# A decoder layer on one core: the second norm written in a fixed order on all engines, between the first products of two gate/up pairs, and four left operands split inside the attention's last steps

## The chip, the cores and the metric

The kernel runs on one core of a Trainium2 chip. The time is the device time of one execution in microseconds (us); a lower one is better. TensorE is written PE, VectorE DVE, ScalarE ACT, GpSimd POOL, and SP is the engine that issues most of the loads.

## What is computed

One decoder layer on x of 512 tokens by 1024 features, all in fp32. An input norm and a projection feed four groups of attention heads; their outputs stand side by side in `mix` and go through `w_out`. Then, cut to what matters here:

```python
x = x + _rms_norm(mix @ w_out[l], attn_post_norm[l])
h = _rms_norm(x, ffn_pre_norm[l])
x = x + _rms_norm(_conv_ffn(h, ffn_w_gate[l], ffn_w_up[l], ffn_conv_w[l], ffn_conv_b[l], ffn_w_down[l]),
                  ffn_post_norm[l])
```

`_conv_ffn` multiplies h by `w_gate` and by `w_up` (1024 by 4096 each), runs a causal convolution of width 3 and a gelu on the gate branch, multiplies the two and goes through `w_down`. The first two lines, from `mix @ w_out` on, and the first products with `w_gate` and `w_up` are what the change touches.

## The kernel before

**Numbers as pairs.** Every matrix operand is held as two fp32r tiles, a rounded copy "hi" and the rest "lo". The copy is made by ACT (line 181 for weights, 1210 for activations), the rest by a DVE subtraction (lines 184, 1211). A product is three matmuls: hi·hi, hi·lo, lo·hi (lines 397 to 399 for the projections, 1263 to 1265 for gate and up).

**Gate and up.** The columns of `w_gate` and `w_up` are taken in 16 pairs, 1 MB of each per pair. One pair is multiplied by a seven-product scheme: the weights' blocks 11, 12, 21, 22 and sums of them are the *left operands* (`operand`, j from 0 to 6, two tiles of hi and two of lo each, 8 instructions on ACT and DVE for two operands), and blocks of h and sums of them, transposed on PE, are the *right operands* R["21"], R["11"], R["t3"], R["t1"], R["t2"], R["t4"], R["22"] (`right_operand`). The sums of weights ("combos") are POOL subtractions and additions of 128 x 512 on line 167: 8 per pair. A product is 24 matmuls.

**The order of the work.** Most of it is placed by a scheduler that goes by the order of issue and by priorities (`tc.high_priority`). The attention runs by a list of events; between them matmuls of the projections (`fill`) fill PE, and small jobs of the other engines wait in a queue (`later`, `pop`, `flush`). After the last event the program runs `flush()`, then the *rest of the output projection*: `out_rest(t, n)` for token block t (0 to 3) and half n (0, 1), 12 matmuls of 128 x 512 each, the last group of heads' share of `mix` among them. Its sums go into `part[t][n]` (line 1168). Four loads of x are issued from ACT's queue at line 1155.

**The second norm** (`second_norm(t)`, `rstd2`) stands behind that for each t: two squares on ACT (line 1176) over the halves of `part[t]`, a root on POOL (1182), a multiplication by the gain (1192, on POOL but for t = 0), the sum with x (1195, DVE), a square over all 1024 columns, a second root, and the multiplication by root and second gain (1198, DVE). Token blocks 0 and 1 give R["11"] and R["21"]; with them the first two products of pairs 0 and 1 run (`first_products`, twice). `other_operands` makes eight differences of the normalised blocks (line 1235, six on DVE and two on POOL, as `TS` says) and the other five right operands, and `other_products` runs the remaining products.

**Left operands at hand.** `W.spare` names two left operands (j = 0 and 1 of pair 0) that have tiles of their own; their 8 splits are popped after the attention. The other operands use slots in turn.

## Time and profile before

| | |
|---|---|
| median of 3 runs | 821.67 us (821.47 to 822.93) |
| the profiled execution | 821.43 us, its span 819.6 us, 1.83 us around the span |
| busy share of the span | PE 95%, DVE 80%, ACT 54%, POOL 42% |
| attention ends (last attention product) | about 265.8 us |
| rest of the output projection on PE | to 282.9 us |
| first gate/up product starts | 298.2 us |

The table's last three lines are read from the timeline of PE. A row of a timeline gives the start in us, the length of the whole group, the engine, the line, the operation, output <- input and the count; in brackets the engine's idle time before it and the instruction that ended this. A row of a window gives for each engine its busy time in the stretch, then the granted clock of PE as a share of full speed.

### The profile page before, as it was taken

The numbers are of one execution on the slowest core, as the hardware profiler recorded it, in microseconds if no ns is written. First come the engines' busy times: TensorE is split into PE (matmuls) and PEld (weight loads), VectorE is DVE, ScalarE is ACT, GpSimd is POOL, SyncE is SP. The second block draws the span as 40 slices with busy tenths as digits, with TensorE's granted clock in tenths as the row PEclk, the third lists the DMA queues.
The fourth block names the chain that finished last, engine by engine and source line by source line (L and its number), as shares of the span: only waits on it lengthen the run. The fifth ranks groups of instructions, "written<-read, shape, count | busy, mean of one in ns | idle before, by whom it ended". The sixth has DMA issues, their size and how long they took to land.

```text
span 819.6 us, 13498 instructions
## 1 busy us (share of the span) xinstructions
PE 781.0 (95%) x5079; PEld 711.5 (87%) x5079; DVE 659.2 (80%) x1126; ACT 445.7 (54%) x930; POOL 341.1 (42%) x314
## 2 busy tenths in 40 slices
PE   6999998999999769999999999999999999999996
PEld 5998886998878659988998998998998998998984
DVE  3547669777686999996797797797897987989867
ACT  5557656776776545645554454454354444444532
POOL 5236342337344657343343442451561561563102
PEclk9999998999999969999999999999999999999999
DMA  7274211406321403412114305206116025033112
GB/s 219 61 199 129 58 40 45 119 21 203 111 77 52 154 5 108 147 61 94 52 51 155 104 12 194 84 22 206 52 52 206 12 92 185 21 104 104 63 67 103
DMA packets 72921, 78.77 MB, mean 96 GB/s; under 512 B 7782, under 2 KB 58136, under 8 KB 72856
## 3 DMA queue, kind: packets, MB, share of 16 engines
q1 hardware_dynamic: 71032, 73.71, 29.4%
q10 hardware_dynamic: 1824, 4.20, 1.5%
q8 instruction: 40, 0.66, 0.3%
q14 instruction: 25, 0.20, 0.1%
HBM read 73.71 MB, written 2.10 MB: 92 GB/s over the span
## 4 chain that ended last, share of the span: by engine, by line
PE 62%; DVE 27%; DMA 3%; ACT 3%; issue 3%; POOL 1%; SPq 0%; ACTq 0%; DVEq 0%; POOLq 0%
DVE wu L184 10%; PE mm L397 5%; PE mm L398 4%; PE mm L399 4%; PE tr L398 4%; PE mm L1263 3%; PE mm L1265 3%; PE mm L1264 3%; PE tr L399 3%; PE tr L397 3%; PE sc L1265 3%; PE sc L1264 3%; PE sc L1263 3%; DVE y L1313 3%; PE tr L924 2%
## 5 line engine op out<-in xcount | busy, mean ns | idle before, releaser
L184 DVE TENSOR_TENSOR wu<-pair,wu 128x512 fp32r<-128x512 f32 x188 | 175.7, 970 | 17.1 <-ACT wu L181 16.7
L181 ACT ACTIVATE wu<-pair 128x512 fp32r<-128x512 f32 x188 | 108.6, 622 | 76.5 <-PE sc L1265 19.7
L1265 PE MATMUL mm<-fT,wu 128*128 128x256 f32 x488 | 138.4, 284 | 0.7 <-DVE wu L184 0.7
L1263 PE MATMUL mm<-fT,wu 128*128 128x256 f32 x488 | 138.3, 283 | 0.7 <-ACT mo L1294 0.7
L1264 PE MATMUL mm<-fT,wu 128*128 128x256 f32 x488 | 138.2, 283 | 0.0
L142 ACT ACTIVATE wu<-raw 128x512 fp32r<-128x512 f32 (+2 forms) x126 | 71.3, 609 | 79.1 <-PE sc L1265 29.1
L1264 PE MATMUL sc<-fT,wu 128*128 128x256 f32 x392 | 111.4, 284 | 0.0
L1263 PE MATMUL sc<-fT,wu 128*128 128x256 f32 x392 | 111.2, 284 | 0.0
L1265 PE MATMUL sc<-fT,wu 128*128 128x256 f32 x392 | 111.2, 284 | 0.0
L167 POOL TENSOR_TENSOR sum<-pair 128x512 f32<-128x512 f32 x32 | 48.4, 1515 | 141.2 <-DVE wu L147 60.7
L167 POOL TENSOR_TENSOR pair<-pair 128x512 f32<-128x512 f32 x64 | 104.5, 1643 | 2.0
L167 POOL TENSOR_TENSOR pair<-sum,pair 128x512 f32<-128x512 f32 x32 | 55.9, 1761 | 116.0 <-DVE wu L184 114.2
L147 DVE TENSOR_TENSOR wu<-raw,wu 128x512 fp32r<-128x512 f32 (+2 forms) x95 | 67.8, 728 | 37.4 <-ACT wu L142 37.0
L1263 PEld LDWEIGHTS mm<-fT,wu 128*128 128x128 f32 x488 | 93.6, 192 | 1.2 <-ACT mo L1294 0.9
L1265 PEld LDWEIGHTS mm<-fT,wu 128*128 128x128 f32 x488 | 93.6, 192 | 1.1 <-DVE wu L184 1.1
L1264 PEld LDWEIGHTS mm<-fT,wu 128*128 128x128 f32 x488 | 93.6, 192 | 0.3
L1263 PEld LDWEIGHTS sc<-fT,wu 128*128 128x128 f32 x392 | 75.5, 193 | 0.3
L1264 PEld LDWEIGHTS sc<-fT,wu 128*128 128x128 f32 x392 | 75.5, 192 | 0.4
L1265 PEld LDWEIGHTS sc<-fT,wu 128*128 128x128 f32 x392 | 75.3, 192 | 0.0
L892 POOL TENSOR_SCALAR P<-P,rc 128x128 f32<-128x128 f32 (+2 forms) x80 | 42.6, 552 | 75.0 <-DVE rc L990 29.5
L147 POOL TENSOR_TENSOR wu<-raw,wu 128x512 fp32r<-128x512 f32 (+2 forms) x31 | 42.8, 1384 | 55.1 <-ACT wu L142 48.9
L900 ACT ACTIVATE P<-P,mn 128x128 f32<-128x128 f32 (+2 forms) x96 | 52.0, 543 | 21.1 <-DVE mn L899 20.6
(317 smaller groups left out, 1993.1 us busy)
## 6 DMA issues: line engine op xcount, KB each, us to landing
pair<-in_ffn_w_gate_dram SPq DMA_DIRECT2D x16, 1024.0 KB
pair<-in_ffn_w_up_dram SPq DMA_DIRECT2D x16, 1024.0 KB, 5.3
raw<-in_ffn_w_down_dram SPq DMA_DIRECT2D x32, 512.0 KB, 3.8
raw<-in_w_in_dram SPq DMA_DIRECT2D x14, 512.0 KB, 3.8
raw<-in_w_out_dram SPq DMA_DIRECT2D x8, 512.0 KB, 4.2
raw<-in_w_in_dram SPq DMA_DIRECT2D x10, 256.0 KB, 2.9
x<-in_x_dram SPq DMA_DIRECT2D x4, 512.0 KB, 6.2
x<-in_x_dram ACTq DMA_DIRECT2D x4, 512.0 KB, 8.9
```

The lines of the kernel that those rows point to most:

```text
L142: self.nc.scalar.activation(box["h"][:, sl], box["r"][:, sl], AF.Copy)
L147: eng.tensor_tensor(box["l"][:, sl], box["r"][:, sl], f32(box["h"][:, sl]), op=ALU.subtract)
L167: self.nc.gpsimd.tensor_tensor(block(g, out), block(g, a), block(g, b), op=op)
L181: self.nc.scalar.activation(box["h"][g], block(g, src), AF.Copy)
L184: self.nc.vector.tensor_sub(box["l"][g], block(g, src), f32(box["h"][g]))
L397: pe.matmul(o, lh, rh, start=first, stop=False)
L398: pe.matmul(o, lh, rl, start=False, stop=False)
L399: pe.matmul(o, ll, rh, start=False, stop=last)
L900: act.activation(pi, pi, AF.Exp, bias=mn[:, i:i + 1], scale=-1.0, accum_out=sm[:, i:i + 1])
L1263: pe.matmul(o, wh, rh, start=first, stop=False, skip_group_check=True)
L1264: pe.matmul(o, wh, rl, start=False, stop=False, skip_group_check=True)
L1265: pe.matmul(o, wl, rh, start=False, stop=last, skip_group_check=True)
```

## The change

- `W.spare` has four operands: j = 0, 1 and also j = 2 ("21") and j = 3 (a sum) of pair 0. In the last part of the attention ("draining") `ask_ahead` queues their 16 splits, and five jobs are popped per event. The first four combos of pair 0 are made earlier.
- The x of token blocks 0 and 1 goes into four tiles `xm` by SP before; x of blocks 2 and 3 is loaded by SP. The loads of pair 1's up weights stand behind these.
- The rest of the output projection, the norm, and the first products are written out instruction by instruction, each of them kept in this order (`tc.keep_in_program_order`). Squares are taken per half (16 on ACT in place of 8 and 4 of double width); each root is three POOL instructions (`r` from the first half's sum, plus the second half's, to the power); the gain multiplication goes to POOL for n = 0 and to DVE for n = 1; all eight differences are on DVE. The differences, t3's, t1's and the further right operands stand between and inside products.
- `mix_pair`'s lo part is on DVE for the last group of heads.

The core of the diff:

```diff
-    W.spare = {W.early: None, W.early + 1: None}
+    W.spare = {W.early + n: None for n in (0, 1, 4, 5)}
...
-        (pool if MLO else vec).tensor_tensor(mixT[1][n], mo, f32(mixT[0][n]), op=ALU.subtract)
+        (pool if n < 6 else vec).tensor_tensor(mixT[1][n], mo, f32(mixT[0][n]), op=ALU.subtract)
...
+        draining = time > now + LAGC - 0.1
+        if draining and "out" not in seen:
+            fill_to("out")
+            flush()
+            W.ask_ahead()
         with tc.high_priority(HP):
             f()
-    fill_to("out")
+            if draining:
+                for _ in range(5):
+                    if side:
+                        pop()
...
+    def squares(t, n, src, c):
...
+        keep(act.activation(junk[:, 0:512], src, AF.Square, scale=1.0 / 32, accum_out=ss[:, n:n + 1]))
+        if n == 0:
+            keep(pool.tensor_scalar(r, ss[:, 0:1], 1.0, EPS, ALU.mult, ALU.add))
         else:
+            keep(pool.tensor_tensor(r, r, ss[:, 1:2], op=ALU.add))
+            keep(pool.tensor_tensor(r, r, mhalf[:, 0:1], op=ALU.pow))
+
+    def half_done(t, n):
+        adds[t, n]()
+        squares(t, n, part[t][n], 0)
+        keep((pool, vec)[n].tensor_tensor(part[t][n], part[t][n], half_of(gpost, n), op=ALU.mult))
+
+    def residual(t, n):
+        xh = half_of(x1[t], n)
+        keep(vec.scalar_tensor_tensor(xh, part[t][n], rms[t, 0][1], f32(xm[t][n]) if t < 2 else xh, ALU.mult, ALU.add))
+        squares(t, n, xh, 1)
+
+    def second_norm(t, n):
+        keep(vec.scalar_tensor_tensor(part[t][n], half_of(x1[t], n), rms[t, 1][1], half_of(gpre, n), ALU.mult, ALU.mult))
...
+    run_all(*(out_rest(t, n) for t in range(2) for n in range(2)))
+    half_done(0, 0)
+    half_done(0, 1)
+    half_done(1, 0)
+    residual(0, 0)
+    residual(0, 1)
+    half_done(1, 1)
+    W.keep = keep
+    run_all(out_rest(2, 0, keep), out_rest(3, 0, keep))
...
+    R["21"], to21 = right_operand([p[0][1], p[1][1]], tags, "M", keep)
+    run_all(g)
+    W.free(2)
+    R["11"], to11 = right_operand([p[0][0], p[1][0]], tags, "M", keep)
+    half_done(2, 1)
+    for f in to21:
+        f()
+    residual(2, 0)
+    half_done(3, 1)
+    residual(2, 1)
+    for f in to11:
+        f()
...
-    firsts = [first_products(tag) for tag in ("mm", "sc")]
-    with tc.high_priority(HN):
-        other_operands()
+    firsts = [first_products("mm", None, keep)]
+    for _ in range(4):
+        pop()
+    residual(3, 0)
+    residual(3, 1)
+    second_norm(2, 1)
+    second_norm(2, 0)
+    for _ in range(4):
+        pop()
+    less(p[0][0], p[2][0], p[0][0], keep)
+    less(p[2][0], p[2][1], p[2][0], keep)
+    firsts[0][2]()
+    second_norm(3, 0)
+    second_norm(3, 1)
+    less(p[1][0], p[3][0], p[1][0], keep)
+    less(p[3][0], p[3][1], p[3][0], keep)
+    todo = []
+
+    def third():
+        R["t3"], f = right_operand([p[2][0], p[3][0]], tags, "H", keep)
+        todo.extend(f)
+    firsts.append(first_products("sc", third, keep))
```

`product` calls `between` after a given number of its matmuls, so t3's transposes stand behind 18 of the 24 matmuls of the fourth product.

**PE, end of the attention.** `va` holds the last attention product (operands `PT`, `vs`), `mixh` and `mixl` the hi and lo of `mix`, `mm` and `sc` the accumulators of `out_rest`. Before:

```order
L1090 MATMUL va_498_3067<-PT_493_3032,vs_1821 128x128
L397 MATMUL mm_517_3179<-wu28_3043,mixh_479_2973 128x512
L398 MATMUL mm_517_3179<-wu28_3043,mixh_479_2973 128x512
L397 MATMUL mm_518_3193<-wu28_3043,mixh_479_2973 128x512
L398 MATMUL mm_518_3193<-wu28_3043,mixh_479_2973 128x512
L397 MATMUL sc_519_3207<-wu30_3129,mixh_479_2973 128x512
L398 MATMUL sc_519_3207<-wu30_3129,mixh_479_2973 128x512
L397 MATMUL sc_520_3221<-wu30_3129,mixh_479_2973 128x512
```

Now:

```order
L1104 MATMUL va_517_3149<-PT_509_3120,vs_1821 128x128
L1104 MATMUL va_517_3149<-PT_510_3121,vs_1821 128x128
L1202 MATMUL mm_529_3201<-wu28_3020,mixh_519_3163 128x512 x2
L1202 MATMUL sc_530_3214<-wu30_3085,mixh_519_3163 128x512 x2
L1202 MATMUL mm_531_3227<-wu28_3020,mixh_519_3163 128x512 x2
L1202 MATMUL sc_532_3240<-wu30_3085,mixh_519_3163 128x512 x2
L1202 MATMUL mm_529_3201<-wu28_3020,mixl_520_3164 128x512
```

Before, 12 matmuls of the head group before the last (`mixh_479`, `mixl_480`) stand between the last attention product and the first matmul on its result (`mixh_500`); now those stand ahead of it, and the matmul on the result (`mixh_519`) follows it directly.

**DVE, from the normalised blocks to t3's operand.** `part` are the blocks of h, `r` the roots, `gains` the second gain, `fT` the right operands, `wu` a left operand's lo, `c` a product's result. Before:

```order
L1198 SCALAR_TENSOR_TENSOR part_487_3010<-x1_3_3171,r_564_3402,gains_2633 128x512
L1198 SCALAR_TENSOR_TENSOR part_516_3160<-x1_3_3171,r_564_3402,gains_2633 128x512
L1235 TENSOR_TENSOR part_423_2729<-part_473_2938,part_423_2729 128x512
L1235 TENSOR_TENSOR part_454_2855<-part_487_3010,part_454_2855 128x512
L1235 TENSOR_TENSOR part_473_2938<-part_504_3109,part_473_2938 128x512
L1235 TENSOR_TENSOR t2_573_3540<-part_504_3109,part_423_2729 128x512
L1235 TENSOR_TENSOR part_487_3010<-part_516_3160,part_487_3010 128x512
L1235 TENSOR_TENSOR t2_574_3541<-part_516_3160,part_454_2855 128x512
L1284 TENSOR_TENSOR c_565_3407<-tmp_568_3478,mm_566_3408 128x2x256
L1211 TENSOR_TENSOR fT_577_3556<-tr_575_3550,fT_576_3555 128x512
```

Now:

```order
L186 TENSOR_TENSOR wu34_3499<-pair33_1_3196,wu34_3499 128x512
L1263 TENSOR_TENSOR part_424_2729<-part_475_2942,part_424_2729 128x512
L1263 TENSOR_TENSOR part_475_2942<-part_495_3065,part_475_2942 128x512
L1340 TENSOR_TENSOR c_577_3430<-tmp_584_3506,mm_578_3431 128x2x256
L1230 SCALAR_TENSOR_TENSOR part_489_3014<-x1_3_3193,r_581_3488,gains_2633 128x512
L1230 SCALAR_TENSOR_TENSOR part_497_3090<-x1_3_3193,r_581_3488,gains_2633 128x512
L1263 TENSOR_TENSOR part_456_2859<-part_489_3014,part_456_2859 128x512
L1263 TENSOR_TENSOR part_489_3014<-part_497_3090,part_489_3014 128x512
L1246 TENSOR_TENSOR fT_591_3575<-tr_588_3558,fT_590_3574 128x512
L1246 TENSOR_TENSOR fT_593_3579<-vb_589_3563,fT_592_3578 128x512
```

The splits of pair 1's second left operand (`wu34`), two of the differences and a result's sum now stand ahead of the last two multiplications by the root.

**POOL, behind the last root.** `pair33` are the weights of pair 1, `sum` their sum. Before:

```order
L1182 TENSOR_TENSOR r_557_3382<-r_557_3382,mhalf_106 128x1
L1182 TENSOR_TENSOR r_564_3402<-r_564_3402,mhalf_106 128x1
L167 TENSOR_TENSOR sum_608_3712<-pair33_0_2640 128x512
L167 TENSOR_TENSOR sum_609_3717<-pair33_1_2642 128x512
L1235 TENSOR_TENSOR part_496_3059<-part_496_3059,t2_573_3540 128x512
L167 TENSOR_TENSOR pair33_0_2640<-pair33_0_2640 128x4x128
L1235 TENSOR_TENSOR part_502_3094<-part_502_3094,t2_574_3541 128x512
```

Now:

```order
L1216 TENSOR_TENSOR r_581_3488<-r_581_3488,ss_580_3487 128x1
L1217 TENSOR_TENSOR r_581_3488<-r_581_3488,mhalf_106 128x1
L166 TENSOR_TENSOR sum_627_3794<-pair33_0_2640 128x512
L166 TENSOR_TENSOR sum_628_3799<-pair33_1_3196 128x512
L166 TENSOR_TENSOR pair33_0_2640<-pair33_0_2640 128x4x128
L166 TENSOR_TENSOR pair33_1_3196<-pair33_1_3196 128x4x128
L166 TENSOR_TENSOR pair33_0_2640<-sum_627_3794,pair33_0_2640 128x4x128
```

Before, two differences of the norm (line 1235, they wait for DVE's `t2`) stand between the combos of pair 1; now all eight combos follow the last root in one row, and none of them waits for DVE's differences.

## Rows read from the trace of the kernel before

**Rows 1.** The page: busy time by engine; chain that ended last.

```profile
PE 781.0 (95%) x5079; PEld 711.5 (87%) x5079; DVE 659.2 (80%) x1126; ACT 445.7 (54%) x930; POOL 341.1 (42%) x314
...
PE 62%; DVE 27%; DMA 3%; ACT 3%; issue 3%; POOL 1%; SPq 0%; ACTq 0%; DVEq 0%; POOLq 0%
```

**Rows 2.** Windows (stretch, length, busy us and instructions per engine, PEclk, DMA).

```profile
240.00:250.00 10.00, 8.84 (x51) 6.32 (x52) 9.68 (x39) 8.19 (x29) 3.16 (x8) 1.00 0.17 52
...
255.00:260.00 5.00, 4.02 (x34) 3.54 (x33) 3.32 (x7) 2.19 (x4) 3.61 (x6) 1.00 0.00 0
...
285.00:290.00 5.00, 0.53 (x2) 0.29 (x2) 5.00 (x9) 3.59 (x9) 1.80 (x2) 0.77 0.00 0
290.00:295.00 5.00, 0.85 (x3) 0.29 (x2) 5.00 (x7) 0.55 (x2) 5.00 (x5) 0.50 0.00 0
...
325.50:345.00 19.50, 18.90 (x157) 18.91 (x158) 17.62 (x27) 13.48 (x23) 4.46 (x3) 1.00 0.57 185
```

**Rows 3.** Timeline, PE, 282 to 299 us (start, length, operation, idle before, releaser).

```profile
282.48 0.39 PE L399 MATMUL sc<-wu,mixl 128*128 128x512 f32 x1
289.48 0.48 PE L1208 MATMUL tr<-ident,part 128*128 128x128 f32 x1 [6.61 <-DVE part L1198]
...
295.31 0.90 PE L1208 MATMUL tr<-ident,part 128*128 128x128 f32 x3 [3.47 <-DVE part L1198]
...
298.18 0.80 PE L1263 MATMUL mm<-fT,wa 128*128 128x256 f32 x2
```

**Rows 4.** Timeline, PE, 322 to 327 us: end of the seventh product.

```profile
325.01 0.28 PE L1264 MATMUL mm<-fT,wu 128*128 128x256 f32 x1
325.13 0.28 PE L1265 MATMUL mm<-fT,wu 128*128 128x256 f32 x1
326.10 0.38 PE L1263 MATMUL mm<-fT,wu 128*128 128x256 f32 x1 [0.69 <-ACT mo L1294]
```

**Rows 5.** Timeline, PE, 264 to 271 us: last attention product, out projection.

```profile
264.52 1.25 PE L1090 MATMUL va<-PT,vs 128*128 128x256 f32 x10
...
268.41 0.39 PE L397 MATMUL mm<-wu,mixh 128*128 128x512 f32 x1
...
270.22 0.62 PE L399 MATMUL mm<-wu,mixl 128*128 128x512 f32 x2
```

**Rows 6.** Timeline, ACT and DVE, 265 to 273 us: last fold, operand splits.

```profile
265.81 0.59 ACT L945 ACTIVATE tmp<-va 64x512 f32<-64x512 f32 x1 [1.32 <-PE va L1090]
...
267.17 0.63 ACT L950 ACTIVATE mixh<-mo 128x512 fp32r<-128x512 f32 x1 [0.76 <-DVE mo L946]
...
268.32 2.20 ACT L181 ACTIVATE wa<-pair 128x512 fp32r<-128x512 f32 x4 [0.52 <-issue]
...
268.98 1.94 DVE L184 TENSOR_TENSOR wa<-pair,wa 128x512 fp32r<-128x512 f32 x3 [1.85 <-ACT wa L181]
```

**Rows 7.** Timeline, DVE and POOL, 276 to 306 us: operations on SBUF tiles.

```profile
294.50 1.41 DVE L1198 SCALAR_TENSOR_TENSOR part<-x,r,gains 128x512 f32<-128x512 f32 x2
...
301.08 4.81 DVE L1198 SCALAR_TENSOR_TENSOR part<-x,r,gains 128x512 f32<-128x512 f32 x4
...
300.50 1.73 POOL L1182 TENSOR_TENSOR r<-r,mhalf 128x1 f32<-128x1 f32 x2 [4.85 <-DVE r L1181]
302.20 3.14 POOL L167 TENSOR_TENSOR sum<-pair 128x512 f32<-128x512 f32 x2
...
276.78 1.29 POOL L1192 TENSOR_TENSOR part<-part,gains 128x512 f32<-128x512 f32 x1
```

**Rows 8.** Timeline, single lengths: a square, a PSUM subtraction, four transposes.

```profile
277.26 0.61 ACT L1176 ACTIVATE junk<-part 128x512 bf16<-128x512 f32 x1
...
298.49 0.68 DVE L1211 TENSOR_TENSOR fT<-tr,fT 128x512 fp32r<-128x512 f32 x1
...
310.50 0.60 PE L1208 MATMUL tr<-ident,part 128*128 128x128 f32 x4
```

**Rows 9.** Windows, 287 to 306 us (columns as in rows 2).

```profile
288.00:301.00 13.00, 7.02 (x28) 5.71 (x29) 13.00 (x21) 6.87 (x16) 7.42 (x7) 0.50 0.01 2
```

More of the change, by code (lines that the diff above doesn't have):

```diff
@@ L53 @@
 GF = (3,)
-GV = (0,)
 PLO = (1,)
-MLO = 1
-TS = (3,)
 RAWS = 2
@@ L166, in combine, with fetch @@
                 q["s", g] = self.sum(late)
-            self.nc.gpsimd.tensor_tensor(block(g, out), block(g, a), block(g, b), op=op)
-        def hi(g):
-            if j == 0:
+            hold = self.pin if late else self.keep
+            hold(self.nc.gpsimd.tensor_tensor(block(g, out), block(g, a), block(g, b), op=op))
+        def fetch(g):
+            if g not in q:
                 while (u, g) not in self.raw:
@@ L195, in operand @@
             return sums + steps
-        return steps + sums if j == 1 and not late else steps
+        if j == "sums":
+            return [lambda: fetch(0), lambda: fetch(1)] + sums[0:4]
+        if j == 1 and not late:
+            return steps + sums[4 if n in self.spare else 0:]
+        return steps
     def ask(self):
@@ L201, in ask, with ask_ahead @@
             self.split += 1
-            self.later(*self.units[self.split - 1]())
+            if self.split - 1 not in self.ahead:
+                self.later(*self.units[self.split - 1]())
+    def ask_ahead(self):
+        for u in sorted(self.ahead):
+            self.later(*self.units[u]())
     def take(self):
@@ L821, in fill_out @@
         W.open_pairs(vpool)
-        W.spare = {u: lambda: [tt("wa", "H") for _ in range(2)] for u in W.spare}
+        W.spare = {u: lambda tag=("H" if u < W.early + 2 else "F"): [tt("wa", tag) for _ in range(2)] for u in W.spare}
+        W.ahead = set(W.spare)
+        later(*W.operand(pairs[0][0], "sums", None, pairs[0][1], False))
         for n in range(2):
@@ L1153, with half_of @@
     x1 = [fp.tile([128, D], F32, name=f"x1_{t}") for t in range(4)]
-    for t in range(4):
-        act.dma_start(x1[t], x[0, 128 * t:128 * t + 128, :])
+    for t in (2, 3):
+        sp.dma_start(x1[t], x[0, 128 * t:128 * t + 128, :])
+    W.done("pair")
     t2pool = ctx.enter_context(tc.tile_pool(name="t2", bufs=XB))
     gpost, gpre = gains[0][:, 0, :], gains[0][:, 1, :]
+    keep = tc.keep_in_program_order
     flush()
     ws = [W.take() for _ in range(4)]
-    def out_rest(t, n):
+    def half_of(a, n):
+        return a[:, 512 * n:512 * n + 512]
@@ L1215, in right_operand @@
-        return hi, lo
-    R = {}
-    for half in range(2):
-        for n in range(2):
-            for t in (2 * half, 2 * half + 1):
-                out_rest(t, n)
-            if half:
-                W.free(2)
-        for t in (2 * half, 2 * half + 1):
-            with tc.high_priority(HN):
-                second_norm(t)
-        if not half:
-            R["11"] = right_operand([part[0][0], part[1][0]], ("tr", "pv"), "M")
-            R["21"] = right_operand([part[0][1], part[1][1]], ("tr", "pv"), "M")
@@ new lines, in split @@
+            def split(ps=ps):
+                h, l = (t2pool.tile([128, S], F32R, tag="X", name=nm("fT")) if tag == "X" else tt("fT", tag)
+                        for _ in range(2))
+                hold(act.activation(h, ps, AF.Copy))
+                hold(vec.tensor_sub(l, ps, f32(h)))
+                for k in range(2):
+                    hi.append(h[:, 256 * k:256 * k + 256])
+                    lo.append(l[:, 256 * k:256 * k + 256])
+            todo.append(split)
+        if hold is keep:
+            return (hi, lo), todo
@@ new lines, in right_operand, with run_all, less @@
+        for f in todo:
+            f()
+        return hi, lo
+    def run_all(*gens):
+        for g in gens:
+            for _ in g:
+                pass
+    def less(o, a, b, hold=lambda i: i, eng=vec):
+        hold(eng.tensor_tensor(o, a, b, op=ALU.subtract))
+    R = {}
+    p = part
+    tags = ("tr", "pv")
+    run_all(*(out_rest(t, n) for t in range(2) for n in range(2)))
[5 more added lines that the diff above has]
+    half_done(1, 1)
@@ L1253, in acc_of, with product @@
         return acc[t // 2][:, 1024 * (t % 2):1024 * (t % 2) + 1024]
-    def product(ps, r, start):
+    def product(ps, r, start, between=None, hold=lambda i: i, at=(0, 2)):
         w = W.take()
@@ L1260, in product @@
             for k in range(4):
+                if between and (g, k) == at:
+                    between()
                 first, last = start and g == 0 and k == 0, k == 3
                 wh, wl, rh, rl = w[0][g][:, k, :], w[1][g][:, k, :], R[r][0][k], R[r][1][k]
[L1263 to L1266 removed]
+                hold(pe.matmul(o, wh, rh, start=first, stop=False, skip_group_check=True))
+                hold(pe.matmul(o, wh, rl, start=False, stop=False, skip_group_check=True))
+                hold(pe.matmul(o, wl, rh, start=False, stop=last, skip_group_check=True))
+                if side and hold is not keep:
                     pop()
@@ L1297, in other_products @@
         bb = bank("mm")
-        product(bb, "t4", True)
+        product(bb, "t4", True, steps[2], hold)
         product(bc, "22", False)
```

152 lines of the change are left out of this document (77 added, 75 removed).

## Prediction

> **What bounds the kernel now.** I read the page first: PE is busy for 95% of the span, and it and DVE carry 62% and 27% of the chain that ended last [rows 1]. In the long run of products PE leaves 0.6 us of 19.5 idle (325.5 to 345 us [rows 2]), so time can only come from a stretch where PE stands still. The windows show one: from 285 to 295 us PE is busy for 1.4 us of 10, while DVE is busy for all of it [rows 2]. The timeline of PE gives its edges: the last matmul of the output projection ends at 282.9, the first product starts at 298.2, and two waits, 6.61 and 3.47 us, end with a DVE multiplication of the second norm [rows 3]. So the norm's DVE and POOL work bounds those 15.3 us. The clock follows: the granted clock is 0.50, the 1.2 GHz level, from 288 to 301 us [rows 9], behind the 6.61 us wait and on past PE's return at 295.3.
>
> I measure the change from one mark to another: Z, the end of the first block's last matmul in `out_rest` (270.6 before: the two matmuls at 270.22 take 0.62 together [rows 5], the first ends about 270.6), and the end of the seventh product, where pair 0's t2 ends (325.45, from the ACT copy behind it, just after the last matmul at 325.13 [rows 4]). Before, Z to the first product is 298.2 - 270.6 = 27.6 us, from there to the end of the seventh product 27.3, together 54.9. Before Z lies the attention, behind the second mark a run that PE fills in both orders.
>
> **The attention's end (Z moves by +4.0).** Eight more splits, 4 of ACT's and 4 of DVE's, and the eight that came after the attention now go into its last part. Before, the splits behind it cost 2.20 us for four on ACT and 1.94 for three on DVE [rows 6], 0.55 and 0.65 each. DVE is busy for 9.68 of 10 us at 240 to 250 [rows 2], so there is no cover for four DVE splits (2.6 us) and two early ones of ACT (1.1) in front of the last softmax: up to +3.7, of which PE can hide about 1.0, its idle time from 255 to 260 [rows 2]. So the last attention product moves by 2.7 to 3.7 beyond the second effect, which is certain in kind: the order puts 12 matmuls ahead of that product that stood behind it. Before, they ran from 265.6 to 268.4 and covered the fold of the last head group, from the ACT copy at 265.81 to the hi copy's end at 267.8 [rows 5, 6]. Now PE waits through the fold: copy 0.6, DVE sum 0.7, hi copy 0.6 and handoffs, 2.1 us. Its lo part on DVE saves nothing there, since PE first has 8 matmuls to do. Ends: if DVE's splits hide altogether, +1.5 (the fold, less idle PE time that the earlier matmuls fill); if nothing hides, 2.1 + 3.7 = +5.8. I take +4.0, nearer the upper end, because of DVE's 9.68 of 10.
>
> **Z to the first product (27.6 before, 18.6 now).** The order on DVE from the first sum to the normalised block that R["21"]'s transposes need has 15 operations of 0.69 us (1.41 for two [rows 7]): 10.3. It waits for squares and roots: a square is 0.75 with its read [rows 8], a root two or three short POOL steps; along the list these waits come to 1.5, 0.2, 1.0, 0.8 and 0.2, together 3.7, and POOL's gain multiplication (1.29 [rows 7]) holds one DVE operation up by 1.0. With 0.3 for the first handoff that is Z + 15.4. Eight transposes at 0.15 (four in 0.60 [rows 8]) give 16.6, one square ahead on ACT 0.9, a hi copy and half its neighbour 1.1: 18.6. PE meanwhile runs the second half of the projection, 42 matmuls of 0.23, and waits twice, 0.9 and 3.9 us. No wait is as long as the 6.61 that preceded the fall of the clock [rows 3, 9], so I leave it at 1.00. This part gives **-9.0**.
>
> **First product to the end of the seventh (27.3 before, 39.6 now).** Products cost 24 x 0.12 = 2.88 (matmuls start 0.12 apart [rows 4]); seven are 20.2. 32 transposes are 4.8. Three waits come on top.
> - R["11"]: its hi copies stand on ACT behind the squares of block 2, which wait for DVE's sum with x; they and the lo end 3.5 us after the first product: **3.5**.
> - t3's transposes, behind 18 matmuls of the fourth product. PE is there at 18.6 + 2.9 + 3.5 + 2.9 + 2.9 + 2.2, about Z + 32.9. They need DVE's 23rd operation counted from R["21"]'s lo, which starts at Z + 18.0. These 23 take 15.3 (eight of 0.62, fifteen of 0.69); waits for a square and a hi copy add 2.5. Without anything else they end at Z + 35.8. But POOL's eight combos of pair 1 now start right behind the last root, about Z + 31.5, and stand against the last eight of them. The rows show what this costs: four multiplications took 4.81 us beside two POOL sums (3.14 us), where two alone took 1.41 [rows 7]: (4.81 - 2.82) / 2 = 1.0 for each POOL operation that comes between, in turns. Five full turns and two partial ones: 5.4. So Z + 41.2, and PE waits 1.8 and 6.6, in all **8.4**. Before, the first differences met no combo, since POOL's own list waited for DVE's `t2`.
> - Others, like the 0.69 that PE waits for a result's copy [rows 4]: **0.7**.
> - The clock: a wait of 6.6 us, as long as the one before 288 us, should bring the 0.50 level again; that one lasted some 6 us past PE's return at 295.3 [rows 3, 9]. Part of this falls on waits. I take **2.0**, ends 0 and 3.
>
> 20.2 + 4.8 + 3.5 + 8.4 + 0.7 + 2.0 = 39.6, so **+12.3**.
>
> About this lock, the Trainium skill, "SBUF — State Buffer", "SBUF: two separate sides", says that a DVE operation with two inputs in SBUF and a POOL operation exclude each other for the whole instruction; the trace agrees, by 1.0 us per turn. By that rule a PSUM input spares DVE, and the PSUM subtractions, 0.68 each [rows 8], fit; so t3's own lo parts stand outside the count.
>
> **What costs nothing.** The loads of x on SP and the later loads of the third pair: x of blocks 2 and 3 is first used at Z + 19.6, the third pair behind the seven products. The 16 half squares in place of 8 and 4 wide ones are ACT work, and ACT is busy for 0.55 of 5 us at 290 to 295 [rows 2]. All differences on DVE add two operations, 1.4 us, counted above where they lie ahead of t3; the other pair comes inside later products.
>
> **The sum.** +4.0 - 9.0 + 12.3 = +7.3. Against the profiled execution, 821.43 us and 0.2 under the median, that is **828.7 us**.
>
> **The rivals.**
> 1. *The weave works.* The 15.3 us of idle PE is filled and the later waits stay small. Then POOL's combos and its gain multiplications don't hold DVE (a turn falls in DVE's waits for roots): -5.4 for the combos, -2.1 for the first block, -2.0 for the clock; 58.2 - 9.5 = 48.7 from Z, -6.2; with the attention's end at +2.7 it is 817.9 us. For it: PE's idle time is real and large [rows 2, 3], and DVE has gaps. Against: the price of a turn [rows 7]. It decides from where under half of the turns hit. The Trainium skill, "Perfetto Trace Analysis", "Optimization Strategy", says that interleaving regimes with different busiest engines may improve performance; the two regimes are there in rows 2, so this rule speaks for this rival.
> 2. *Only the combos miss.* The combos come late, say as their loads land late, and the rest is as forecast: 7.3 - 5.4 - 2.0 = -0.1, 821.3 us.
> 3. *The attention's end is worse.* Nothing is hidden and the clock falls for longer: +5.8 and 3.0 in place of 4.0 and 2.0: 831.5 us.
>
> **How the numbers follow.** A difference under 0.2%, 1.6 us, can't be told from none. The forecast with its own bounds (+1.5 to +5.8 at the attention's end, 0 to 3 for the clock) lies from 824.2 to 831.5: chance 0.52. Rival 1 has 0.24, since DVE may catch its roots differently than my list does; rival 2 0.12, rival 3 0.12. So faster 0.24, same 0.12, slower 0.64. The range goes from 817.5, just under rival 1, to 832.0, just over rival 3: about 2 in 10 lie outside, runs of rival 1 with a smaller end of the attention first.
>
> **What would show it.** Right: the first product starts some 21 to 25 us after 270.6 and so earlier than 298.2 (near 293); PE's longest wait after it is at the transposes of t3, 6 to 7 us, ended by a DVE difference, beside an unbroken row of POOL combos; the DVE operations there take 1.7, not 0.7; PE idles about 2 us just before the last heads' matmuls. Wrong: t3's transposes start less than 3 us behind the fourth product's 18th matmul (rival 1 or 2), or the last attention product ends before 269 (the splits were hidden), or PE has new waits behind the seventh product, which I put at nothing.

## The result, and the profile after

The changed kernel takes 833.42 us (median of 4 runs, 829.78 to 835.22) beside 822.30 for the kernel before (4 runs): a ratio of 1.013, with a 95% interval of 1.0106 to 1.0154. It is slower, as forecast, but by 11 us and not 7.3, above the range's end of 832.0. The profiled execution took 829.78 us (span 828.0), the lowest of the four, and 8.35 over that of before. Four more runs of the same kernel gave 829.13 to 835.82 (ratio 1.0125, 1.0084 to 1.0165), and their profile, of a run of 835.82 us, shows the same waits but for one (R["11"], below): its attention reached its last quarter 3.9 us later (235.2 against 231.2 us at the 76th exponential). So a mark inside the attention separates that spread from the change, and the table of the experiments uses it.

The waits of PE, from the timeline of the changed kernel (start, length, operation, idle before and what ended it):

```profile
274.30 0.73 PE L1202 MATMUL mm<-wu,mixh 128*128 128x512 f32 x2 [2.07 <-ACT mixh L964]
...
289.61 0.30 PE L1240 MATMUL tr<-ident,part 128*128 128x128 f32 x1 [1.55 <-DVE part L1230]
...
291.64 0.90 PE L1240 MATMUL tr<-ident,part 128*128 128x128 f32 x3 [1.73 <-DVE part L1230]
...
297.29 0.36 PE L1317 MATMUL mm<-fT,wa 128*128 128x256 f32 x1
...
310.39 0.30 PE L1240 MATMUL tr<-ident,part 128*128 128x128 f32 x1 [1.21 <-DVE part L1263]
...
316.98 0.90 PE L1240 MATMUL tr<-ident,part 128*128 128x128 f32 x3 [6.29 <-DVE part L1263]
...
352.40 0.38 PE L1317 MATMUL mm<-fT,wu 128*128 128x256 f32 x1 [1.39 <-DVE tmp L1354]
```

The first row is the fold's wait, 2.07 us. It had no match before: there the 12 matmuls from 265.6 on covered it [rows 5]. The transposes of R["21"] then wait 1.55 and 1.73, where before PE waited 6.61 and 3.47 [rows 3], and the first product starts at 297.29, 0.9 us earlier than 298.18. t3's transposes wait 1.21 and 6.29, and the last row is a wait that before did not have.

What stands behind the 6.29, on DVE and POOL of the changed kernel:

```profile
306.77 3.47 DVE L1263 TENSOR_TENSOR part<-part,part 128x512 f32<-128x512 f32 x2
...
310.77 2.82 DVE L1230 SCALAR_TENSOR_TENSOR part<-x,r,gains 128x512 f32<-128x512 f32 x2
313.51 3.42 DVE L1263 TENSOR_TENSOR part<-part,part 128x512 f32<-128x512 f32 x2
...
306.63 3.07 POOL L166 TENSOR_TENSOR sum<-pair 128x512 f32<-128x512 f32 x2
309.66 3.38 POOL L166 TENSOR_TENSOR pair<-pair 128x512 f32<-128x512 f32 x2
313.00 3.37 POOL L166 TENSOR_TENSOR pair<-sum,pair 128x512 f32<-128x512 f32 x2
316.34 2.95 POOL L166 TENSOR_TENSOR pair<-pair 128x512 f32<-128x512 f32 x2
```

DVE's differences and multiplications take 1.7, 1.4 and 1.7 us each (two per row), beside an unbroken row of POOL's combos; alone two took 1.41 [rows 7].

The same kernel in windows (stretch, length, busy us and instructions of PE, PEld, DVE, ACT and POOL, the granted clock, DMA):

```profile
240.00:250.00 10.00, 8.50 (x34) 6.35 (x34) 8.99 (x33) 6.59 (x24) 2.64 (x6) 0.66 0.12 47
255.00:260.00 5.00, 5.00 (x24) 4.08 (x24) 2.97 (x13) 1.74 (x7) 2.97 (x4) 0.66 0.09 30
291.60:297.30 5.70, 5.66 (x22) 4.98 (x22) 4.39 (x7) 2.67 (x7) 3.32 (x5) 0.50 0.01 3
310.00:315.00 5.00, 0.30 (x1) 0.14 (x1) 5.00 (x5) 0.00 (x0) 5.00 (x4) 0.93 0.04 14
315.00:320.00 5.00, 3.02 (x14) 3.02 (x15) 3.18 (x4) 1.19 (x2) 5.00 (x4) 0.50 0.61 196
```

From 240 to 250 us the granted clock is 0.66 on average and from 255 to 260 too, where before it was 1.00 in both windows [rows 2]. That is new, and inside the attention. From 291.6 us to the first product it is 0.50, where the forecast had 1.00. Behind the long wait at t3 it is 0.50, as forecast.

The end of the seventh product is 331.92 us:

```profile
331.92 0.60 ACT L1353 ACTIVATE mo<-mm 128x512 f32<-128x512 f32 x1 [1.50 <-PE mm L1319]
```

It was 325.45 before, so 6.5 of the 8.4 us lie ahead of it and 1.9 behind.

### The profile page after: what moved, and what is told of

Same layout as the page of the kernel before. It is cut to its first block, busy times and chain, and to the rows that moved or that the text cites. A ratio compares the mean times of both kernels' runs of the same rounds, so it can differ in the third digit from the quotient of the medians.

```text
span 828.0 us, 13538 instructions
## 1 busy us (share of the span) xinstructions
PE 786.8 (95%) x5079; PEld 716.7 (87%) x5079; DVE 658.2 (80%) x1124; ACT 446.3 (54%) x938; POOL 340.6 (41%) x324
## 4 chain that ended last, share of the span: by engine, by line
PE 32%; DVE 24%; issue 3%; DMA 2%; ACT 1%; POOL 1%; DVEq 0%; POOLq 0%; ACTq 0%
DVE wu L186 11%; DVE y L1372 3%; PE tr L410 3%; PE mm L1317 3%; PE mm L1319 3%; PE mm L1318 3%; PE tr L411 3%; PE sc L1319 2%; PE sc L1318 2%; PE sc L1317 2%; PE tr L409 2%; DMA pair<-in_ffn_w_up_dram 1%; PE va L409 1%; DVE y L1375 1%; PE va L410 1%
## 5 line engine op out<-in xcount | busy, mean ns | idle before, releaser
L186 DVE TENSOR_TENSOR wu<-pair,wu 128x512 fp32r<-128x512 f32 x186 | 166.9, 933 | 15.7 <-ACT wu L183 15.4
L1317 PE MATMUL mm<-fT,wu 128*128 128x256 f32 x480 | 136.2, 284 | 2.1 <-DVE tmp L1354 1.4
L1319 PE MATMUL mm<-fT,wu 128*128 128x256 f32 x480 | 136.0, 283 | 0.2 <-DVE wu L186 0.2
L1318 PE MATMUL mm<-fT,wu 128*128 128x256 f32 x480 | 135.8, 283 | 0.0
L1319 PE MATMUL sc<-fT,wu 128*128 128x256 f32 x384 | 108.9, 284 | 0.0
L1318 PE MATMUL sc<-fT,wu 128*128 128x256 f32 x384 | 108.8, 284 | 0.0
L1317 PE MATMUL sc<-fT,wu 128*128 128x256 f32 x384 | 108.8, 284 | 0.0
L166 POOL TENSOR_TENSOR pair<-sum,pair 128x512 f32<-128x512 f32 x32 | 59.9, 1887 | 111.0 <-DVE wu L186 105.9
L166 POOL TENSOR_TENSOR pair<-pair 128x512 f32<-128x512 f32 x64 | 102.8, 1618 | 2.0
L1317 PEld LDWEIGHTS mm<-fT,wu 128*128 128x128 f32 x480 | 92.1, 192 | 2.7 <-DVE tmp L1354 1.6
L1319 PEld LDWEIGHTS mm<-fT,wu 128*128 128x128 f32 x480 | 92.1, 192 | 0.5 <-DVE wu L186 0.4
L1318 PEld LDWEIGHTS mm<-fT,wu 128*128 128x128 f32 x480 | 92.1, 192 | 0.3
L1318 PEld LDWEIGHTS sc<-fT,wu 128*128 128x128 f32 x384 | 74.0, 193 | 0.3
L1317 PEld LDWEIGHTS sc<-fT,wu 128*128 128x128 f32 x384 | 73.9, 193 | 0.4
L1319 PEld LDWEIGHTS sc<-fT,wu 128*128 128x128 f32 x384 | 74.0, 193 | 0.0
L914 ACT ACTIVATE P<-P,mn 128x128 f32<-128x128 f32 (+2 forms) x96 | 52.1, 544 | 24.9 <-DVE mn L913 24.4
```

The source lines that it names most:

```text
L166: hold(self.nc.gpsimd.tensor_tensor(block(g, out), block(g, a), block(g, b), op=op))
L186: self.keep(self.nc.vector.tensor_sub(box["l"][g], block(g, src), f32(box["h"][g])))
L914: act.activation(pi, pi, AF.Exp, bias=mn[:, i:i + 1], scale=-1.0, accum_out=sm[:, i:i + 1])
L1317: hold(pe.matmul(o, wh, rh, start=first, stop=False, skip_group_check=True))
L1318: hold(pe.matmul(o, wh, rl, start=False, stop=False, skip_group_check=True))
L1319: hold(pe.matmul(o, wl, rh, start=False, stop=last, skip_group_check=True))
```

## The experiments

All stretches below are read from the timelines of one profile each: A, from the 76th to the 96th (last) exponential of the attention; B, to the end of the last attention product; C, to the first gate/up product; D, to the ACT copy behind the seventh product; E, to a wait of 1.1 us of PE that every kernel has early in the steady run. From there to the end all take 453.2 to 454.8 us. The sums are those of the rounded entries. The ratio is that of the times, with its 95% interval.

| kernel | A | B | C | D | E | sum | ratio to before |
|---|---|---|---|---|---|---|---|
| before | 21.2 | 12.2 | 32.4 | 27.3 | 40.6 | 133.7 | 1 |
| changed | 25.7 | 15.3 | 25.1 | 34.6 | 42.7 | 143.4 | 1.0130 (1.0106 to 1.0154) |
| changed, again | 26.3 | 15.6 | 23.8 | 36.9 | 42.7 | 145.3 | 1.0125 (1.0084 to 1.0165) |
| combos behind t3 | 25.3 | 15.3 | 25.1 | 34.5 | 42.7 | 142.9 | 1.0149 (1.0118 to 1.0179) |
| splits queued late | 25.3 | 15.3 | 28.6 | 34.6 | 42.7 | 146.5 | 1.0166 (1.0141 to 1.0192) |
| last product first | 26.0 | 12.8 | 24.5 | 35.2 | 42.7 | 141.2 | 1.0092 (1.0063 to 1.0120) |
| norm alone | 21.2 | 12.2 | 28.6 | 38.5 | 42.7 | 143.2 | 1.0118 (1.0102 to 1.0135) |
| attention's end alone | 25.8 | 15.3 | 27.6 | 27.7 | 40.6 | 137.0 | 1.0051 (1.0033 to 1.0069) |
| combos behind t4 | 26.6 | 14.6 | 24.9 | 29.9 | 45.6 | 141.6 | 1.0104 (1.0072 to 1.0137) |
| norm alone, combos behind t4 | 21.2 | 12.2 | 28.3 | 32.5 | 45.6 | 139.8 | 1.0065 (1.0050 to 1.0080) |
| splits behind the softmax, old norm | 21.2 | 12.7 | 32.4 | 27.2 | 40.6 | 134.1 | 1.0002 (0.9989 to 1.0016) |
| the same, new norm, combos behind t4 | 21.2 | 12.7 | 29.0 | 28.7 | 45.5 | 137.1 | 1.0033 (1.0020 to 1.0045) |
| gains on DVE, old kernel | 21.2 | 12.2 | 31.2 | 27.3 | 40.6 | 132.5 | 0.9970 (0.9957 to 0.9983) |
| no combos of pair 1 | 26.4 | 15.6 | 23.8 | 31.4 | 42.5 | 139.7 | 1.0050 (1.0033 to 1.0068) |

**The changed kernel again.**

> The changed kernel once more, for its own spread: 829.8 to 835.2 us in four runs, and the profile that was taken is that of the fastest. If the spread comes from PE's granted clock in the attention, another profile shows 0.50 stretches of another length before 262 us; if it comes from late loads of gate/up weights, it shows new waits of PE or DVE behind the seventh product, at the same clock.

The two profiles differ by 6.1 us. A to E come to 145.3 us, 1.9 over the first profile, and 3.9 us lie ahead of A. Of these, 2.2 lie between the 36th and the 41st exponential, where PE's clock is down in the second profile and not in the first. Here is the first profile, and then the second:

```profile
135.00:140.00 5.00, 3.64 (x19) 2.69 (x17) 4.86 (x14) 4.61 (x14) 0.00 (x0) 1.00 0.24 71
```

```profile
135.00:140.00 5.00, 4.29 (x14) 3.09 (x12) 4.86 (x14) 4.62 (x14) 0.00 (x0) 0.54 0.26 76
```

Another 1.6 lie between the 61st and the 66th exponential, with the clock at 1.00 in both. So the first guess, PE's clock in the attention, holds for about half of what lies ahead of A. Loads behind the seventh product are not it: E is 42.7 in both. Why C is shorter and D longer in the second profile is told below, with the first product.

**Pair 1's combos behind t3's differences.** A one-column POOL operation reads the last difference of t3 ahead of them:

```diff
     less(p[3][0], p[3][1], p[3][0], keep)
+    gate = st.tile([128, 1], F32, tag="gate", name=nm("gate"))
+    keep(pool.tensor_scalar(gate, p[3][0][:, 0:1], 1.0, EPS, ALU.mult, ALU.add))
```

> The eight combos of pair 1 on POOL wait for the last of t3's four differences (a one-column POOL operation reads its result ahead of them). Theory (turns between POOL's combos and DVE's last operations): DVE's operations there fall from 1.7 to 0.7 us each, PE's waits at t3's transposes from 1.2 and 6.3 us to under 2 together, the 0.50 clock behind them goes, and the time falls by 5 to 7.5 us against the changed kernel. Rival (DVE's list is too long by itself, or POOL only reaches the combos when DVE is through): the wait falls by under 1.5 us and the time by as little.

The operations ahead of t3 fell to 0.7 us each and of the waits of 1.21 and 6.29 one of 2.20 is left, but D stayed at 34.5: the turns had moved. DVE in this kernel, with the differences of t2 and of t4:

```profile
315.57 3.36 DVE L1263 TENSOR_TENSOR t<-part,part 128x512 f32<-128x512 f32 x2
...
323.45 3.46 DVE L1263 TENSOR_TENSOR part<-part,t 128x512 f32<-128x512 f32 x2
```

and PE:

```profile
318.99 0.55 PE L1240 MATMUL tr<-ident,t 128*128 128x128 f32 x3 [1.29 <-DVE t L1263]
...
325.38 0.30 PE L1240 MATMUL tr<-ident,part 128*128 128x128 f32 x1 [1.54 <-DVE part L1263]
...
326.96 0.55 PE L1240 MATMUL tr<-ident,part 128*128 128x128 f32 x3 [1.28 <-DVE part L1263]
```

Two differences that took 1.3 us in the changed kernel take 3.4 beside the combos, and PE now waits for t2's and t4's operands: with the 2.20 at t3 and 0.75 for a lo part, 7.1 us in place of 7.5. The clock is 0.50 again behind these waits (from 328 to 331 us). The rival's number came out, for a reason that neither theory had.

**The splits queued late.** The five jobs per event of the attention's last part are taken out:

```diff
-            if draining:
-                for _ in range(5):
-                    if side:
-                        pop()
```

> The four left operands' 16 splits are queued behind the attention's last steps again, not inside them. Theory (the splits hold up DVE and ACT in the attention and so leave PE idle, which also brings the 0.50 clock): last attention product 3 to 5 us earlier, granted clock 1.00 from 240 to 262 us, the splits now beside the out projection; time 2 to 4 us below the changed kernel. Rival (the clock and the delay come from the projection's matmuls being used up ahead of the last steps): the 0.50 stretches stay, the last attention product moves by under 1.5 us.

It told nothing of the splits: A stayed at 25.3, since the scheduler moved the splits of t3's and t1's left operands, whose sources are there early, ahead of the last softmax by itself, and others went beside the norm, where C grew by 3.5 us. The time rose by some 3 us, where the theory had it fall by 2 to 4.

**The last attention product ahead of the 12 matmuls.**

```diff
+                with (tc.issue_after(last_pv[0].ins) if t < 2 and k == 2 else ExitStack()):
+                    hold(pe.matmul(ps, mixT[a][4 + k][:, sl], w[c][:, k % 2, :], start=k == 0 and a == c == 0,
+                                   stop=k == 3 and a == 1))
```

> The 12 matmuls of the out projection on the head group before the last stand behind the last attention product again. Theory: PE's 2.07 us wait for the last fold goes, and the time falls by about 2 us. Rival (the norm's chain on DVE and POOL starts no earlier or is held by another wait): the wait goes, the time falls by under 0.7 us.

The wait went and A to E fell by 2.2 us; the median fell from some 833 to 830.6. The theory held, though the two ratios' intervals just overlap.

**Each half of the change alone.** The norm alone has the old end of the attention:

```diff
-    W.spare = {W.early + n: None for n in (0, 1, 4, 5)}
+    W.spare = {W.early + n: None for n in (0, 1)}
...
-        draining = time > now + LAGC - 0.1
-        if draining and "out" not in seen:
-            fill_to("out")
-            flush()
-            W.ask_ahead()
...
+    fill_to("out")
```

> The norm and the first products in the new order, the attention's end as before: two left operands, split behind the attention, the projection's matmuls not used up ahead of the last steps. Theory (four DVE splits inside a stretch that DVE already fills make PE wait there, and its clock falls to 0.50 twice): from the 76th to the 96th exponential it takes 21 to 22 us as before, not 25 to 26, no 0.50 stretch lies between 240 and 262 us, the 2.07 us wait of the last fold is gone, and the time is 5 to 8 us under the changed kernel, some 825 to 828. Rival (the fall of the clock is chance, as in other places of the attention): under 3 us.

The attention's end alone is the reverse: the kernel before with the four spare operands, their early combos and the draining block (the same lines with the signs turned round).

> The reverse: the kernel before, with four left operands split inside the attention's last steps. Theory: from the 76th to the 96th exponential 25 to 26 us, a 2 us wait for the last fold, 0.50 stretches ahead of 262 us; time 4 to 7 us over the kernel before, some 827 to 830. It gains at most the four splits that no longer stand beside the norm (1 to 2 us). Rival (the attention's end costs nothing by itself): within 1.6 us of before.

For the attention's end both runs say the same: A is 21.2 without it and 25.8 with it, and the fold's wait is there with it (2.07 us in the trace of the attention's end alone) and not without. B's 3.1 are mostly the 12 matmuls (2.8), which leave C. Windows of the attention's end alone:

```profile
240.00:250.00 10.00, 8.41 (x35) 5.94 (x35) 8.97 (x30) 7.13 (x25) 3.81 (x6) 0.75 0.16 54
250.00:262.00 12.00, 10.80 (x57) 8.84 (x55) 9.38 (x35) 8.27 (x28) 4.49 (x8) 0.78 0.28 88
```

The same windows of the kernel with the splits behind the softmax (its edit is below):

```profile
240.00:250.00 10.00, 9.06 (x55) 6.58 (x53) 9.68 (x40) 8.02 (x30) 3.16 (x7) 1.00 0.15 52
250.00:262.00 12.00, 9.88 (x70) 8.26 (x70) 10.24 (x29) 9.28 (x26) 8.29 (x14) 1.00 0.29 89
```

With the splits inside, PE's clock is down for part of the time (0.75 and 0.78 on average); without them it is 1.00. But the sum did not follow: the norm alone is at 832 us, 1.4 under the whole change, not 5 to 8. The left operands of t3 and t1 now have to be split beside the norm. C is 3.5 longer, of which the 12 matmuls are 2.8 and the missing fold wait -2.1, so 2.8 are splits; D is 3.9 longer, with PE waiting 1.25 us for ACT's split and 0.41 for DVE's, and a second stretch at 0.50 behind these waits (from 321.4 to 324.8 us). What the early splits cost in the attention they save later almost whole.

**The combos behind t4's last difference.**

```diff
                 less(*combine(t), keep)
+            if name == "t4":
+                gate = st.tile([128, 1], F32, tag="gate", name=nm("gate"))
+                keep(pool.tensor_scalar(gate, p[1][1][:, 0:1], 1.0, EPS, ALU.mult, ALU.add))
```

Once in the changed kernel, once in the norm alone.

> The eight combos of pair 1 wait for the last difference of t4, so none stands beside a difference that a right operand needs. The gate behind t3's differences only moved the turns on to those of t2 and t4 (3.4 us for two each). Theory (the turns are the price, wherever they fall): from the first product to the end of the seventh 28 to 30 us, not 34.6; time 4 to 6 us under the changed kernel. Rival (then the combos are late for pair 1's own operands, or DVE's splits pay for them): the seventh product ends 5 us earlier, but PE waits as long before the first product of pair 1 or of the next pair, and the time falls by under 2 us.

> The two together: the old end of the attention, the new norm, pair 1's combos behind the last difference of t4. If both theories hold the savings add up: 9 to 14 us under the changed kernel, some 819 to 824, at best 3 us under the kernel before. If the combos' lock only moves on, it is within 2 us of the norm alone.

D fell as the theory has it, to 29.9, and E rose from 42.7 to 45.6: pair 1's own operands are late, as the rival has it. PE behind the seventh product:

```profile
336.94 0.39 PE L1319 MATMUL mm<-fT,wu 128*128 128x256 f32 x1 [0.25 <-DVE wu L186]
...
342.61 0.39 PE L1319 MATMUL sc<-fT,wu 128*128 128x256 f32 x1 [2.27 <-DVE wu L186]
...
352.13 0.39 PE L1317 MATMUL mm<-fT,wu 128*128 128x256 f32 x1 [1.10 <-DVE tmp L1354]
```

1.8 us are left of 4.7, and the median falls by some 3, between the theory's 4 to 6 and the rival's 2. With the old end of the attention it comes to 1.0065, the best of the written norm so far, but 827.6 us are 5.8 under the changed kernel and not the 9 to 14 of the expectation: the savings do not add up.

**The splits behind the last softmax.** The ACT and DVE splits of the four operands are queued behind the last exponential of the sink and the sum that takes it in, at normal priority.

```diff
+            with self.after('vec'):
+                self.keep(self.nc.vector.tensor_sub(box["l"][g], block(g, src), f32(box["h"][g])))
...
+            W.marks["act"] = act.activation(es, mn, AF.Exp, bias=sink[:, h:h + 1]).ins
+            W.marks["vec"] = vec.tensor_add(sm, sm, es).ins
```

> The kernel before with four left operands split at the attention's end, but none of the 16 splits ahead of the last softmax (queued behind its last ACT and DVE instruction, at normal priority), and the projection's matmuls not used up early. Theory (DVE is full ahead of the last softmax and half idle behind it, so it is the place of the splits that costs, not their number): from the 76th to the 96th exponential 21 us as before, the last attention product within 1 us of before, no 2 us wait for the last fold; and the norm, freed of four splits, gets to the first product 3 to 5 us earlier, so 817 to 820 us, 2 to 4 under the kernel before. Rival (the splits in the idle part delay the folds, or the freed time is lost to the combos' turns): within 1.6 us of before.

> The changed kernel's norm and weave, with the splits behind the last softmax and pair 1's combos behind t4's last difference. Theory: attention's end as before, last product to first product some 24 us in place of 32.4, then 30 and 45.6 us as with the late combos: 24 - 32.4 + 30 - 27.3 + 45.6 - 40.6 = about -1, so 820 to 823 us. Rival (the wait only moves: DVE's work from the attention's end to the next pair is the same and the written order leaves it idle in places): 824 or more.

The place was the cost: A is 21.2 with all four operands, and B 12.7 (this kernel does not use up the projection's matmuls early either). With the old norm C stayed at 32.4 to the tenth all the same. DVE does 12 splits there in both kernels: where two operands' splits had gone, the scheduler put the next two's. So the theory was right on the place and wrong on the time: 822.31 us beside 822.51, as the rival has it. With the new norm this is 2.5 us over before, the rival's "824 or more".

**Gains on DVE.** In the kernel before:

```diff
-GV = (0,)
+GV = (0, 1, 2, 3)
```

> The kernel before with all eight gain multiplications on DVE, not six of them on POOL. Theory (a POOL operation on SBUF tiles costs DVE 1.0 us when it comes between, more than the 0.6 to 0.7 that the multiplication takes on DVE): the first product starts 1 to 3 us earlier and the time falls by 0.5 to 2 us. Rival (few of the six meet a DVE operation with two SBUF inputs, so DVE gets 4 us of work for less than that): the first product 1 to 3 us later.

820.14 us (10 runs), against 822.51: C falls by 1.2 us, and the other stretches are as before. Where the other half of the 2.4 us comes from, these stretches do not show. DVE in this kernel:

```profile
276.16 1.70 DVE L1192 TENSOR_TENSOR part<-part,gains 128x512 f32<-128x512 f32 x1
277.78 1.40 DVE L1195 SCALAR_TENSOR_TENSOR x<-part,r,x 128x512 f32<-128x512 f32 x2
...
282.79 1.40 DVE L1195 SCALAR_TENSOR_TENSOR x<-part,r,x 128x512 f32<-128x512 f32 x2
```

The first multiplication still meets a combo (1.70), but the sums with x take 1.40 for two, twice. In the kernel before the first two of them took 3.40, beside a POOL multiplication and a combo:

```profile
276.93 3.40 DVE L1195 SCALAR_TENSOR_TENSOR x<-part,r,x 128x512 f32<-128x512 f32 x2
```

This version beats both kernels.

**No combos of pair 1.** In `combine`:

```diff
+            if late:
+                q["s", g] = block(g, "21")
+                return
             if out == "s":
```

> The changed kernel without the eight POOL combos of pair 1 (pair 1 is multiplied by its plain blocks in their place, so this part of the computation is left out). It tells what the combos' turns cost in all, with nothing moved on. Theory (they are the wait at t3 and more than half of what came behind the seventh product): first to seventh product 27 to 30 us in place of 34.6, and from there to the mark of the steady run 40.6 to 41.5 in place of 42.7; 6 to 9 us under the changed kernel. Rival (DVE's written list is what is late, the combos only fill its gaps): first to seventh product above 32 us, under 3 us in all.

The total is the theory's, the places are not: the median is 826.4 against 833.1 and 833.4, about 7 us less, but D is 31.4 and E 42.5, above what it gave them. The profile to compare with is the second one of the changed kernel, which like this one has no stretch at 0.50 between Z and the first product (C is 23.8 in both). Beside it D and E are some 5.6 us less, the 0.50 stretch behind t3's long wait included. PE still waits 2.20 at t3 and 1.28 at t2, with DVE free of POOL:

```profile
316.72 0.55 PE L1243 MATMUL tr<-ident,part 128*128 128x128 f32 x3 [2.20 <-DVE part L1266]
...
324.37 0.55 PE L1243 MATMUL tr<-ident,t 128*128 128x128 f32 x3 [1.28 <-DVE t L1266]
```

So the turns, with the clock that falls behind them, are over half of the second profile's excess in D (36.9 against 27.3), and some 3.5 us of waits come from DVE's own list.

## Why the prediction was right and wrong

**Right: direction, place and mechanism.** The fold's wait was forecast at 2.1 us and is 2.07; the wait at t3's transposes 1.8 and 6.6, measured 1.21 and 6.29, ended by a DVE difference beside an unbroken row of combos, with DVE's operations at 1.4 to 1.7 us and the 0.50 clock behind. The six operations that stand there against the combos took 9.7 us in place of 4.2 (the same six in the run with the combos behind t3's differences), so the turns came to 5.5 where I had 5.4. The first product was forecast near 293 and came at 297.29, still ahead of 298.18.

**The attention's end: +4.0, measured +6.0, and this step failed.** Z is at about 276.6 us (the first matmul on `mixl` behind the fold starts at 276.24 and takes 0.39) in place of 270.6; and since this execution reached the 76th exponential 1.1 us earlier than that of before, the change itself costs 7.1, more than the upper bound of 5.8. I had the four DVE splits and two of ACT ahead of the last softmax at 3.7 and let PE hide 1.0. Nothing was hidden: A is 4.1 to 5.4 over that of before in the eight profiles that have them. The cover that I named, PE's idle time from 255 to 260 us [rows 2], lies behind that softmax, so nothing ahead of it could use it. The least, 4.1, stands where the clock is 1.00 almost to the end of A (the run with the combos behind t3's differences), so the 3.7 was too small even without the clock; the longest A have the longest stretches at 0.50. Here is A before, and then in that run:

```profile
232.30:253.60 21.30, 18.79 (x109) 14.52 (x108) 20.28 (x74) 19.08 (x62) 10.00 (x17) 1.00 0.31 99
```

```profile
231.50:256.80 25.30, 20.12 (x112) 14.90 (x111) 23.30 (x79) 21.23 (x66) 10.15 (x15) 0.99 0.40 126
```

DVE's busy time grows by 3.0 us and ACT's by 2.2, which is four splits on each (2.8 and 2.6) within what else shifts; PE's matmuls grow by three. No run has the splits out of A and the projection's matmuls used up early, so no run tells these two apart; the busy times speak for the splits.

**Z to the first product: 18.6, measured 20.7, and here the clock failed.** -9.0 became -6.9. My list of DVE was right: its block for the last transposes of R["21"] is there at Z + 15.0 (forecast 15.4), and the second hi copy ends at Z + 18.0. But I left the clock at 1.00, as no wait was as long as the 6.61 of before. It fell all the same, at the two waits of 1.55 and 1.73 us, and PE then worked without a break up to the first product at 0.50. In the second profile, with the same two waits, the same 22 matmuls ran at 1.00 (the row at 0.50 is among the windows above):

```profile
297.80:300.90 3.10, 3.03 (x22) 2.72 (x22) 2.25 (x5) 1.70 (x4) 2.80 (x4) 1.00 0.00 0
...
278.80:282.10 3.30, 2.98 (x7) 2.40 (x8) 1.68 (x1) 0.27 (x1) 1.44 (x2) 0.50 0.97 362
```

There the first product starts at Z + 18.0, under the forecast's 18.6.

**First product to the end of the seventh: 39.6, measured 34.6.** t3's 8.4 was 7.5 and the clock behind it some 2, as said; the 0.7 for other waits lies behind the mark. The wait for R["11"], 3.5, was 0.34. The second profile has it at 2.35 and 0.34. Here is the first profile, and then the second:

```profile
301.13 0.38 PE L1318 MATMUL mm<-fT,wa 128*128 128x256 f32 x1 [0.34 <-DVE fT L1246]
```

```profile
306.64 0.38 PE L1317 MATMUL mm<-fT,wa 128*128 128x256 f32 x1 [2.35 <-ACT fT L1245]
307.36 0.38 PE L1318 MATMUL mm<-fT,wa 128*128 128x256 f32 x1 [0.34 <-DVE fT L1246]
```

In both, PE goes on with R["11"]'s lo part at Z + 24.5 (forecast 25.0). So what the clock took ahead of the first product came off this wait, and cost nothing in the end. These two errors are one wait at two places: 18.6 + 3.5 against 20.7 + 0.34. From Z to the end of the seventh product the change costs 0.4 us, where I had 3.3.

**Behind the seventh product: nothing, measured +1.9 (E: +2.1), and this step failed too.** Eight transposes, 1.2 us, moved behind my second mark, since R["22"] is now made inside the product behind it: 40 lie between the first product and the mark before, and 32 now. I priced the 32 and put nothing behind the mark. And PE waits 1.39 us at 352.40 for a DVE sum. I had listed new waits there as a way to be wrong and given them nothing.

**The median.** +6.0 - 6.9 + 7.3 + 1.9 = +8.3 gives the profiled execution's 829.8, inside the range, but this is luck: +2.0 and +1.9 of errors stand against -2.9. The runs' median lies 3.6 above that execution, and the kernel before's profiled execution was 0.9 below its own median of 822.3; I measured against one execution and left no room for it. The second profile shows what a longer execution has: 2.2 us from the clock's stretch at 135 us, 1.6 ahead of the 66th exponential, and 2.3 from the 76th exponential to Z, 1.4 of them behind the last attention product, where PE is at 0.50 right behind the fold (the second row of its windows above). Why such a stretch falls in one execution and not in another was not tried.

**Rivals.** The attention's end alone is worth 4 us (1.0051), and rival 3, which made it the worst case, came nearest. Rival 2 was tested: with the combos out of t3's way nothing is gained (142.9 against 143.4), as their turns fall on the next differences, so its -7.4 was wrong in kind: a lock's price does not go when its first victim is spared. The Trainium skill, "Perfetto Trace Analysis", "Optimization Strategy", says that interleaving regimes may help where the most-contended engine changes from one to the other. The trace does not bear it out here, because DVE was full in both regimes. These are windows of the kernel before, from the last attention product to the first gate/up product and from there to the end of the seventh, and of the changed one up to its first product:

```profile
265.80:298.20 32.40, 20.89 (x89) 16.15 (x88) 29.89 (x41) 17.52 (x38) 21.31 (x17) 0.84 0.28 97
298.20:325.50 27.30, 26.75 (x208) 25.97 (x208) 27.30 (x36) 13.62 (x26) 20.34 (x14) 0.94 0.17 53
```

```profile
272.20:297.30 25.10, 19.11 (x78) 15.02 (x77) 18.50 (x24) 10.85 (x29) 17.26 (x24) 0.86 0.25 84
```

DVE is busy for 29.9 of 32.4 us and for all of the next 27.3 before, its turns with POOL included, and for 18.5 of 25.1 now. PE's idle time there was no free room: the scheduler had filled DVE's waits with 12 splits that the next products need, and the written order has none there. It starts the products earlier and leaves DVE idle for 6.6 us in its waits for the fold, for squares and for roots. PE then waits for DVE's list behind the first product: even without POOL's combos, 2.20 us at t3 and 1.28 at t2.

## What to carry to other kernels

An idle PE was a gain here only as far as the engine that it waits for had work removed, not moved: sum DVE's busy time over the whole stretch before ordering PE's work into the gap. Work that went into a place where the engine was already full cost its length, and more where PE's clock then fell; the same 16 splits cost 0.5 us behind the last softmax (and brought nothing there either, while DVE's list behind them stayed full). Before a late mark is called a cost, look at the wait behind it: counted from Z, the first product came 2.7 us later in one execution of the changed kernel than in the other and cost nothing, since the next wait ended at the same time in both. And where DVE and POOL took turns, moving POOL's operations mostly picked who waits; putting six of POOL's multiplications on DVE gave 0.3%.

## What the runs showed of the hardware that was not expected

PE's granted clock can fall in one execution and not in another of the same order of instructions. The changed kernel's two profiles show it ahead of the first product: 5.66 us for 22 matmuls at 0.50, 3.03 for the same 22 at 1.00. The attention shows it too. In the changed kernel it was 0.66 on average from 240 to 250 us, and PE's 8.50 busy us there are long because its matmuls then take longer. In the run with the combos behind t3's differences, whose attention is the same, it stayed at 1.00 up to 256 us, with PE busy for 5.55 of 8:

```profile
240.00:248.00 8.00, 5.55 (x28) 3.50 (x28) 7.85 (x27) 5.16 (x19) 2.17 (x4) 1.00 0.17 64
248.00:256.00 8.00, 6.17 (x42) 4.86 (x41) 7.16 (x25) 7.57 (x26) 1.73 (x4) 1.00 0.42 132
256.00:260.00 4.00, 4.00 (x17) 3.16 (x17) 1.84 (x9) 0.79 (x3) 3.10 (x4) 0.57 0.00 0
```

A was 25.3 there and 25.7 in the changed kernel, so most of A's excess over 21.2 is not the clock's. What tips the clock stays open.
